# Layer 1's attention: the shared rotary key reaches the other key tiles by SBUF-to-SBUF transfers

## The chip, the cores and the metric

The kernel runs on one core of a Trainium2 chip. The metric is the device time of one execution in microseconds (us), the median of repeated runs. Engines are named as in the profile: PE is TensorE (matmuls and transposes), DVE is VectorE, ACT is ScalarE, POOL is GpSimd, and SP is SyncE, which only issues DMAs in this kernel.

## The reference

The model is a trunk of two layers over one sequence of 1024 tokens with 1024 features, all in float32. Layer 0 is a differential attention, layer 1 a multi-head latent attention (MLA); a gated MLP with a causal convolution follows each. The change touches layer 1's attention:

```python
proj = h @ w_in
c_q = rms_norm(proj[..., :MLA_Q_RANK], q_norm_g)
c_kv = rms_norm(proj[..., MLA_Q_RANK:MLA_Q_RANK + MLA_KV_RANK], kv_norm_g)
k_pe = apply_rope(proj[..., MLA_Q_RANK + MLA_KV_RANK:], cos, sin)
q = (c_q @ w_uq).reshape(b, s, MLA_HEADS, MLA_NOPE + MLA_ROPE)
q_pe = apply_rope(q[..., MLA_NOPE:], cos, sin)
kv = (c_kv @ w_ukv).reshape(b, s, MLA_HEADS, MLA_NOPE + MLA_V)
...
sc = (jnp.einsum('bqhd,bkhd->bhqk', qn, k_nope)
      + jnp.einsum('bqhr,bkr->bhqk', qp, k_pe)).astype(jnp.float32) * scale
```

There are 16 heads. Each has 64 key features of its own (`k_nope`), but the 32 rotary key features (`k_pe`) have no head index: all heads use the same ones. A chunk mask (chunks of 64 tokens) and a softmax follow, then the product with the values.

## The kernel before

**Parts of a number.** A float32 matmul operand is held as a high part (`hi`, L123 to L127: a cast to F32R, on ACT unless DVE is asked for) and a low part (`lo`, L130: the difference, on DVE unless POOL is asked for). `mm3` (L119 to L121) makes a product of three matmuls. Tiles live in named places of SBUF: `s0` to `s13` (8 KB in each partition), `u0` to `u15` (4 KB) and `h0` to `h13` (2 KB). A new tile in a place waits until the last user of the old one is done.

**The key tiles.** A key tile `kT[j]` has 128 partitions, and in each the high and the low part for 1024 tokens. Partitions 0 to 63 hold the head's own key features. Partitions 64 to 127 hold the rotary key, twice (64 to 95 and 96 to 127), which answers to the two rotated forms of the query in `q`. There are four tiles, in `s0`, `s11`, `s12` and `s8`; head n uses tile n mod 4. The own features are written anew for each pair of heads (`k_unit`), but the rotary half of a tile is written once and stays for all heads. `rotary` writes it into `kT[0]` from the rotated key, for one half of the tokens (512) at a time; `share(j, half)` then copies partitions 64 to 127 of such a half from `kT[0]` to `kT[j]`.

**Order of the stage.** `mla_input` runs over the eight token tiles of 128, and two rounds more: `latents(i)` makes the projections and norms of tile i (squares at L157, the root on POOL at L163, the norm at L1293), `turn` transposes them, `values` makes the values and writes them to DRAM (`v_d`). After round 5 `rotary(0)` turns the first half of the key, in round 8 `rotary(1)` turns the second. `heads.first` starts three products of the first pair of heads ahead of the last tile.

Then `steps` runs 64 attention steps, four for each head. A step t has two query blocks of 128; in most heads the four steps take the blocks in the order `p` = 1, 0, 3, 2, so that the first two need keys of the first half alone. Each step computes scores (into the two PSUM tiles `S`), their row maximum (L1625, DVE) and exponential (L1626, ACT), scales the probabilities (`weigh`, L1632 on DVE and L149 on POOL), transposes them (L248, PE) with a split into parts (L127 on ACT, L130 on DVE), and multiplies by the values (L1646 and L1647, PE) into the single PSUM bank `u`, which L1649 (ACT) and L1650 (DVE) empty into SBUF. The work of three steps overlaps. `prepare(t)` puts the fetches and splits of later heads' weights and values among the steps, and there the copies for tiles 2 and 3.

**What sets the order on the engines.** Outside regions that are scheduled by hand (`manual_schedule`, not used in this stage), a planner orders the instructions at build time: the kernel is built with `tile.TileContext(nc, schedule_with_timeline_sim=True)`. It follows a simulated timeline, in which an instruction that is ready earlier can go ahead of others written before it. So the written order is not the order in the queues: two of the copies that `prepare` writes at steps 3 and 5 run at 1326 and 1328 us, before the first exponential of step 0 at 1331.9 us. On the chip each engine works off its queue in the order fixed at build time, and an instruction whose inputs aren't ready holds up what is behind it.

Of the kernel before, what the change touches and what calls it, by code (L numbers as in the profile page):

```python
# [56 lines left out]
class Trunk:  # L57
# [1196 lines left out]
    def mla_input(self, W, hts, turns, v_d, heads_of):  # L1254


        nc, a = self.nc, self.a
# [11 lines left out]
        def latent_tiles(half):  # L1269
            for x, place in zip((cq, ckv), (("s2", "s3"), ("s6", "s7"))[half]):  # L1270
                pieces = self.at(place, [P, 4, 512], F32R)
                for part in range(2):
                    x[part].append(pieces[:, 2 * part : 2 * part + 2, :])
            for part in range(2):
                cq2[part].append(self.at(f"h{2 * half + part}", [P, 512], F32R))
# [7 lines left out]
        def latents(i):  # L1283
            acc = self.big()
            for k in range(KD):
                for b, m, kind in ((0, 384, "q"), (512, 288, "kv")):
                    wh, wl = where[kind, k]
                    self.mm3(acc[:, b : b + m], hts[i][:, 0, k, :], hts[i][:, 1, k, :], wh, wl, k == 0, k == KD - 1)
            nat = nats([P, 672])
            for b, m, off, gain in ((0, 384, 0, g[0]), (512, 256, 384, g[1])):  # L1290
                d = nat[:, off : off + m]
                r = self.rstd(acc[:, b : b + m], d, m)
                nc.vector.scalar_tensor_tensor(d, acc[:, b : b + m], r, gain, ALU.mult, ALU.mult)  # L1293
            nc.scalar.copy(nat[:, 640:672], acc[:, 768:800])
            return nat

        def turn(i, nat):
            half = i // 4
            s = slice((i % 4) * P, (i % 4 + 1) * P)
            ps = self.bank()  # L1300
            for j in range(3):
                nc.tensor.transpose(ps[:, j * P : (j + 1) * P], nat[:, j * P : (j + 1) * P], self.ident)
            v = ps.rearrange("p (k s) -> p k s", s=P)
            for dst, src in ((cq, v[:, 0:2]), (cq2, v[:, 2])):
                h, l = (x[half][:, s] if dst is cq2 else x[half][:, :, s] for x in dst)
                self.hi(h, src)
                self.lo(l, src, h)
            ps = self.bank()
            for j in range(2):
                nc.tensor.transpose(ps[:, j * P : (j + 1) * P], nat[:, (3 + j) * P : (4 + j) * P], self.ident)  # L1310
            nc.tensor.transpose(ps[:MLA_ROPE, 256:384], nat[:, 640:672], self.ident)
            v = ps[:, :256].rearrange("p (k s) -> p k s", s=P)
            self.hi(ckv[0][half][:, :, s], v)
            self.lo(ckv[1][half][:, :, s], v, ckv[0][half][:, :, s])
            nc.scalar.copy(kp[half][:, s], ps[:MLA_ROPE, 256:384])

        def values(i):
            half = i // 4
            s = slice((i % 4) * P, (i % 4 + 1) * P)
            vs = self.raw([P, D])  # L1320
            for b, y in ((0, self.bank("u")), (512, self.bank())):
                for k in range(2):
                    ch, cl = (cT.kv(part, half, k)[:, s] for part in range(2))
                    self.mm3(y, ch, cl, late.wv[k][0][:, b : b + 512], late.wv[k][1][:, b : b + 512], k == 0, k == 1)
                if b == 0:
                    heads.own(i, y[:, :P])
                nc.scalar.copy(vs[:, b : b + 512], y)
            nc.sync.dma_start(v_d[:, :, i].rearrange("h p e -> p h e"), vs.rearrange("p (h e) -> p h e", e=P))

        def fetch_tab(half):  # L1330
            late.tab = [self.at(place, [MLA_ROPE, 512]) for place in ("h12", "h13")]
            for x in range(2):
                nc.sync.dma_start(late.tab[x], a["rope_k"][:, x, half * 512 : (half + 1) * 512])

        def rotary(half):
            r = self.rope(rope, kp[half], *late.tab, MLA_ROPE // 2, MLA_ROPE)
            t = nats([MLA_ROPE, 2, 512], F32R)
            self.hi(t[:, 0, :], r[:MLA_ROPE])
            self.lo(t[:, 1, :], r[:MLA_ROPE], t[:, 0, :], nc.gpsimd)
            heads.rotary(half, t)  # L1340
# [3 lines left out]
        for i in range(NT + 2):  # L1344
            if readies:
                readies.pop(0)()
            if i == NT - 1:
                heads.share(1, 0)
                heads.first()
            if i < NT:  # L1350
                nat[i] = latents(i)
                if turns:
                    turns.pop(0)()
            if i in (1, 5):
                latent_tiles(i // 4)
            if i == 1:

                late.wv = [self.split(f"s{4 + k}", self.fetch(a["mla_wuv"][k * P : (k + 1) * P, :], D)) for k in range(2)]
                heads = heads_of(cT)
            if i == 4:  # L1360
                fetch_tab(0)
            if 0 <= i - 1 < NT:
                turn(i - 1, nat.pop(i - 1))
            if i >= 2:
                values(i - 2)
            if i == 5:
                rotary(0)
                fetch_tab(1)
            if i == NT:
                rotary(1)  # L1370
                heads.share(1, 1)
        return heads

    def mla_heads(self, cT, v_d, o_d):
        nc, a = self.nc, self.a
        pairs = MLA_HEADS // 2
        heads = [dict() for _ in range(MLA_HEADS)]
# [3 lines left out]
        k_places, kT = ["s0", "s11", "s12", "s8"], []  # L1381
# [6 lines left out]
        def fetch_w(p):  # L1388
            raws["w"] = self.fetch(a["mla_w"][p], D)
# [16 lines left out]
        def q_unit(h, half):  # L1406
            if half == 0:
                heads[h]["q"] = q_ring([P, 2, S], F32R)
            q = heads[h]["q"]
            acc = self.bank()  # L1410
            off = (h % 2) * 384
            for k in range(3):
                wh, wl = (w[:, off + k * P : off + (k + 1) * P] for w in W[h // 2])
                self.mm3(acc, wh, wl, cT.q(0, half, k), cT.q(1, half, k), k == 0, k == 2)
            yield
            s = slice(half * 512, (half + 1) * 512)
            t = t_ring([P, 512])
            nc.vector.tensor_mul(t, acc, cs[:, s])
            self.hi(q[:, 0, s], t)
            self.lo(q[:, 1, s], t, q[:, 0, s], nc.gpsimd if h > 1 else None)  # L1420

        def k_unit(p, half):
            acc = self.bank()
            for k in range(2):
                wh, wl = (w[:, 768 + k * P : 768 + (k + 1) * P] for w in W[p])
                self.mm3(acc, wh, wl, cT.kv(0, half, k), cT.kv(1, half, k), k == 0, k == 1)
            yield
            s = slice(half * 512, (half + 1) * 512)
            for j in range(2):
                k = heads[2 * p + j]["k"] = kT[(2 * p + j) % 4]  # L1430
                src = acc[j * 64 : j * 64 + 64]
                self.hi(k[0:64, 0, s], src)
                self.lo(k[0:64, 1, s], src, k[0:64, 0, s])

        def pair_units(p):
            return [
                lambda: k_unit(p, 0), lambda: k_unit(p, 1),
                lambda: q_unit(2 * p, 0), lambda: q_unit(2 * p, 1),
                lambda: q_unit(2 * p + 1, 0), lambda: q_unit(2 * p + 1, 1),
            ]  # L1440
# [3 lines left out]

        def first():

            self.run([u() for u in pair_units(0)[::2]])

        def own(i, y):
# [8 lines left out]
        def k_tiles(n):  # L1458
            kT.extend(self.at(place, [P, 2, S], F32R) for place in k_places[len(kT) : n])
# [5 lines left out]
            for x, r0 in enumerate((64, 96)):  # L1465
                self.hi(kT[0][r0 : r0 + 32, :, s], t, nc.vector if x else None)

        def share(j, half):
            k_tiles(j + 1)
            s = slice(half * 512, (half + 1) * 512)  # L1470
            self.hi(kT[j][64:128, :, s], kT[0][64:128, :, s])

        def prepare(t):
            p, u = divmod(t, 8)
            if t == 0:
                fetch_w(1)
            if t == 1:
                split_w(1)
                k_tiles(4)
            if 3 <= t < 7:  # L1480
                share(2 + (t - 3) // 2, (t - 3) % 2)
            for at, ahead, f in ((2, 1, fetch_v), (4, 1, split_v), (5, 2, fetch_w), (7, 2, split_w)):
                if u == at and p + ahead < pairs:
                    f(p + ahead)
            if t >= 4 * MLA_HEADS - 10:
                prefetch[0]()
# [439 lines left out]
```

## Time and profile before

| | |
|---|---|
| time, median of 3 runs | 2433.61 us (2432.45 to 2436.21) |
| the profiled execution's own time | 2437.63 us |
| its span in the profile | 2435.8 us |
| instructions | 32815 |
| DMA, mean over the span | 88 GB/s |
| HBM read, written | 159.37 MB, 52.43 MB |

The profile shows one execution. Its span runs from the first to the last instruction; its own time is 1.8 us longer. A timeline gives the start of an instruction from the start of the span, its length, its engine and line, the tile it writes and those it reads, and in brackets how long its engine stood idle before it and what ended that. Tiles `S`, `b` and `u` written by PE are PSUM tiles; the names `s`, `u` and `h` written by other engines are the places in SBUF, without their numbers.

### The profile page before, as it was taken

The numbers are of one execution on the slowest core, as the hardware profiler recorded it, in microseconds if no ns is written. First come the engines' busy times: TensorE is split into PE (matmuls) and PEld (weight loads), VectorE is DVE, ScalarE is ACT, GpSimd is POOL, SyncE is SP. The second block draws the span as 40 slices with busy tenths as digits, with TensorE's granted clock in tenths as the row PEclk, the third lists the DMA queues.
The fourth block names the chain that finished last, engine by engine and source line by source line (L and its number), as shares of the span: only waits on it lengthen the run. The fifth ranks groups of instructions, "written<-read, shape, count | busy, mean of one in ns | idle before, by whom it ended". The sixth has DMA issues, their size and how long they took to land. (4 is left out here: it accounts for less than half of the span.)

```text
span 2435.8 us, 32815 instructions
## 1 busy us (share of the span) xinstructions
PE 2366.7 (97%) x12032; PEld 2011.8 (83%) x12032; DVE 1901.7 (78%) x3091; ACT 1304.2 (54%) x2432; POOL 626.4 (26%) x500
## 2 busy tenths in 40 slices
PE   7999999999999999999999999999999999999998
PEld 6888787888888888878898789988888888887886
DVE  6667776856888888899964788886478888888997
ACT  5677777844444444444445777775344444444443
POOL 4545454425000000000042666664330000000001
PEclk9999999999999999999999999999999999999999
DMA  4101111233222222543221211123322222227502
GB/s 161 42 34 44 35 36 44 100 100 120 74 80 78 87 78 93 193 173 122 84 89 54 68 40 40 40 80 116 106 69 87 78 88 86 78 87 276 173 1 78
DMA packets 95505, 213.93 MB, mean 88 GB/s; under 512 B 8688, under 2 KB 33904, under 8 KB 95344
## 3 DMA queue, kind: packets, MB, share of 16 engines
q1 hardware_dynamic: 86448, 184.56, 22.6%
q10 hardware_dynamic: 8896, 27.27, 3.0%
q8 instruction: 95, 1.56, 0.3%
q14 instruction: 66, 0.54, 0.1%
HBM read 159.37 MB, written 52.43 MB: 87 GB/s over the span
## 5 line engine op out<-in xcount | busy, mean ns | idle before, releaser
L163 POOL TENSOR_TENSOR st<-st,mhalf 128x1 f32<-128x1 f32 x56 | 34.3, 614 | 1310.7 <-DVE st L162 1306.8
L127 ACT CAST u<-h 128x512 fp32r<-128x512 f32 (+2 forms) x242 | 146.1, 619 | 279.8 <-DVE h L771 259.9
L119 PE MATMUL S<-s,u 128*128 128x512 f32 (+1 forms) x752 | 286.6, 381 | 0.6 <-DVE s L130 0.5
L121 PE MATMUL S<-s,u 128*128 128x512 f32 (+1 forms) x752 | 285.1, 379 | 0.0
L120 PE MATMUL S<-s,u 128*128 128x512 f32 (+1 forms) x752 | 285.1, 379 | 0.0
L119 PE MATMUL b<-s,u 128*128 128x512 f32 x588 | 230.6, 392 | 2.1 <-DVE S L1624 1.0
L120 PE MATMUL b<-s,u 128*128 128x512 f32 x588 | 229.0, 389 | 0.0
L121 PE MATMUL b<-s,u 128*128 128x512 f32 x588 | 229.0, 389 | 0.0
L828 DVE SCALAR_TENSOR_TENSOR u<-u,conv,u 128x1023 f32<-128x1023 f32 (+1 forms) x176 | 225.0, 1278 | 1.9 <-ACT u L824 1.9
L149 POOL TENSOR_TENSOR u<-u,st 128x384 f32<-128x384 f32 (+7 forms) x160 | 169.7, 1070 | 149.1 <-DVE st L1632 107.2
L119 PE MATMUL u<-s,s 128*128 128x512 f32 (+1 forms) x440 | 177.8, 404 | 13.4 <-ACT h L552 7.1
L127 ACT CAST s<-u 128x512 fp32r<-128x512 f32 (+2 forms) x202 | 128.9, 673 | 101.8 <-PE u L121 36.0
L130 DVE TENSOR_TENSOR u<-b,u 128x512 fp32r<-128x512 f32 (+1 forms) x256 | 158.1, 630 | 29.7 <-ACT u L127 27.9
L121 PE MATMUL u<-s,s 128*128 128x512 f32 (+1 forms) x440 | 172.8, 393 | 0.0
L120 PE MATMUL u<-s,s 128*128 128x512 f32 (+1 forms) x440 | 172.2, 391 | 0.0
L119 PEld LDWEIGHTS S<-s,u 128*128 128x128 f32 x752 | 142.6, 190 | 27.6 <-DVE s L130 0.9
L120 PEld LDWEIGHTS S<-s,u 128*128 128x128 f32 x752 | 142.6, 190 | 26.3
L121 PEld LDWEIGHTS S<-s,u 128*128 128x128 f32 x752 | 142.5, 190 | 26.1
L127 ACT CAST u<-b 128x512 fp32r<-128x512 f32 (+1 forms) x256 | 133.6, 551 | 36.9 <-PE b L248 27.3
L831 ACT ACTIVATE u<-u 128x1024 f32<-128x1024 f32 x44 | 46.7, 1062 | 187.5 <-DVE u L828 187.5
L130 DVE TENSOR_TENSOR u<-h,u 128x512 fp32r<-128x512 f32 x166 | 114.1, 688 | 32.4 <-ACT u L127 31.5
L130 DVE TENSOR_TENSOR s<-u,s 128x512 fp32r<-128x512 f32 (+2 forms) x187 | 127.7, 717 | 11.7 <-ACT s L127 11.5
(260 smaller groups left out, 6641.7 us busy)
## 6 DMA issues: line engine op xcount, KB each, us to landing
u<-in_ffn_up SPq DMA_DIRECT2D x88, 512.0 KB, 3.9
g_d<-u ACTq DMA_DIRECT2D x44, 512.0 KB, 2.6
u<-in_ffn_down SPq DMA_DIRECT2D x66, 256.0 KB, 5.1
u<-g_d SPq DMA_DIRECT2D x62, 256.0 KB, 4.2
s<-in_da_wqkv SPq DMA_DIRECT2D x23, 512.0 KB, 3.2
x_d<-u SPq DMA_DIRECT2D x16, 512.0 KB, 2.9
s<-x_d SPq DMA_DIRECT2D x8, 1024.0 KB, 10.8
u<-o_d SPq DMA_DIRECT2D x24, 256.0 KB, 2.8
```

The source lines that it names most:

```text
L119: mm(out, lh, rl, start=first, stop=False, skip_group_check=onto)
L120: mm(out, lh, rh, start=False, stop=False, skip_group_check=onto)
L121: mm(out, ll, rh, start=False, stop=last, skip_group_check=onto)
L127: self.nc.scalar.copy(out, src)
L130: (eng or self.nc.vector).tensor_sub(out, src, hi.bitcast(F32))
L149: self.nc.gpsimd.tensor_mul(x, x, s.to_broadcast(list(x.shape)))
L163: nc.gpsimd.tensor_tensor(r, s, self.mhalf, ALU.pow)
L828: nc.vector.scalar_tensor_tensor(t[half][:, back:], u[half][:, : S - back], w, t[half][:, back:], ALU.mult, ALU.add)
L831: nc.scalar.activation(t[0], t[0], AF.Silu)
```

## The change

The six copies on ACT (three tiles, two halves of 512 tokens, 64 partitions by 2 x 512 elements each) are replaced by three transfers, one for each tile, of 64 partitions by 2 x 1024 elements, 512 KB each. They are issued by POOL (`nc.gpsimd.dma_start`). Since each covers all tokens, it comes after `rotary(1)`: that for tile 1 is written where the second half copy was, and those for tiles 2 and 3 at step 1, behind the split of the second pair's weights, instead of steps 3 to 6. The place of tile 1 is taken in `heads.first`, at the same point of the order as before; the places of tiles 2 and 3 are taken at step 1, as before.

```diff
@@ mla_input
             if i == NT - 1:
-                heads.share(1, 0)
                 heads.first()
...
             if i == NT:
                 rotary(1)
-                heads.share(1, 1)
+                heads.share(1)
@@ mla_heads
         def first():
 
+            k_tiles(2)
             self.run([u() for u in pair_units(0)[::2]])
...
-        def share(j, half):
+        def share(j):
             k_tiles(j + 1)
-            s = slice(half * 512, (half + 1) * 512)
-            self.hi(kT[j][64:128, :, s], kT[0][64:128, :, s])
+            nc.gpsimd.dma_start(kT[j][64:128], kT[0][64:128])
 
         def prepare(t):
...
             if t == 1:
                 split_w(1)
-                k_tiles(4)
-            if 3 <= t < 7:
-                share(2 + (t - 3) // 2, (t - 3) % 2)
+                share(2)
+                share(3)
```

## The prediction

> **What bounds the kernel now.** I read the page first, then the groups of instructions by form, then the stretch in which the changed lines run (by windows of 4 us, and as a timeline of each engine), then the DMA issues. Of the page:
>
> ```profile
> span 2435.8 us, 32815 instructions
> PE 2366.7 (97%) x12032; PEld 2011.8 (83%) x12032; DVE 1901.7 (78%) x3091; ACT 1304.2 (54%) x2432; POOL 626.4 (26%) x500
> s<-x_d SPq DMA_DIRECT2D x8, 1024.0 KB, 10.8
> ```
>
> PE is busy for 2366.7 of 2435.8 us. An edit that takes no work from PE can only win where PE stands idle or runs at a lower clock, 69 us in the whole span. The edit takes this group away from ACT, and nothing from PE:
>
> ```profile
> L127 ACT CAST s<-s 64x1024 fp32r<-64x1024 f32 x6 | 6.1, 1042 | 5.7 <-PE S L121 5.6
> ```
>
> That is 6.1 us on an engine with a share of 54%, so the share says "free". A share is an average, though, and the six copies all lie between 1310 and 1355 us. The windows of that stretch (columns: length, then busy us of PE, PEld, DVE, ACT and POOL with counts, then the granted PE clock, DMA share, GB/s) show a place where ACT is full and PE isn't:
>
> ```profile
> 1328.00:1332.00 4.00, 3.34 (x16) 2.42 (x16) 3.19 (x10) 3.94 (x13) 1.10 (x2) 1.00 0.00 0
> ...
> 1348.00:1352.00 4.00, 3.16 (x17) 2.29 (x15) 3.52 (x3) 3.95 (x6) 2.76 (x3) 1.00 0.27 108
> 1352.00:1356.00 4.00, 2.12 (x10) 1.51 (x10) 3.50 (x7) 3.91 (x6) 2.13 (x1) 1.00 0.59 184
> 1356.00:1360.00 4.00, 3.42 (x13) 2.83 (x14) 2.83 (x7) 3.92 (x8) 1.68 (x1) 0.68 0.20 80
> 1360.00:1364.00 4.00, 3.37 (x19) 2.53 (x17) 3.67 (x10) 2.37 (x5) 3.11 (x2) 0.89 0.14 33
> ```
>
> PE's idle time in these rows is 0.66 + 0.84 + 1.88 + 0.58 + 0.63 = 4.59 us, and the clock of 0.68 and of 0.89 in two of them costs at most 0.32 x 4 + 0.11 x 4 = 1.72 us more. So 6.3 us is about all that this edit can win here.
>
> **The copies that go.** The timeline of ACT (start, length, instruction, idle time before it and its releaser):
>
> ```profile
> 1310.41 1.04 ACT L127 CAST s<-s 64x1024 fp32r<-64x1024 f32 x1 [2.67 <-PE S L121]
> ...
> 1326.27 1.04 ACT L127 CAST s<-s 64x1024 fp32r<-64x1024 f32 x1 [2.96 <-PE S L121]
> 1327.34 0.49 ACT L157 ACTIVATE u<-S 128x384 f32<-128x384 f32 x1
> ...
> 1328.07 1.05 ACT L127 CAST s<-s 64x1024 fp32r<-64x1024 f32 x1
> ...
> 1349.16 1.04 ACT L127 CAST s<-u 32x1024 fp32r<-32x1024 f32 x1
> ...
> 1352.15 2.94 ACT L127 CAST s<-s 64x1024 fp32r<-64x1024 f32 x3
> 1355.11 0.48 ACT L127 CAST u<-b 128x384 fp32r<-128x384 f32 x1
> 1355.62 0.37 ACT L1649 COPY h<-u 64x256 f32<-64x256 f32 x1
> 1356.01 1.01 ACT L1626 ACTIVATE u<-S,st 128x896 f32<-128x896 f32 x1
> ```
>
> Only the first three copies (the first halves of the three key tiles) come early, each as soon as PE releases a slot. The three second halves follow the rotation of the second half (1349.16) and stand in a row of 2.94 us, ahead of three things that others wait for. PE and DVE at that place:
>
> ```profile
> 1350.26 0.44 PE L119 MATMUL S<-s,s 128*128 128x384 f32 x1 [0.59 <-ACT s L127]
> ...
> 1356.56 0.38 PE L1646 MATMUL u<-u,s 128*128 128x256 f32 x1 [2.29 <-DVE h L1650]
> ...
> 1361.27 0.44 PE L119 MATMUL S<-s,s 128*128 128x384 f32 x1
> ...
> 1361.90 1.55 PE L248 MATMUL b<-ident,u 128*128 128x128 f32 x10
> 1353.96 1.20 DVE L1625 TENSOR_REDUCE st<-S 128x1 f32<-128x1024 f32 x1
> 1355.62 0.56 DVE L130 TENSOR_TENSOR u<-b,u 128x384 fp32r<-128x384 f32 x1 [0.46 <-ACT u L127]
> 1356.10 0.40 DVE L1650 TENSOR_TENSOR h<-h,u 64x256 f32<-64x256 f32 x1
> ```
>
> The product at L1646 needs its one PSUM bank emptied, by L1649 on ACT and then L1650 on DVE. L1649 stands behind the three copies, so PE loses 2.29 us. Without them the cast of 1355.11 and L1649 could run 2.94 us earlier, L1649 at about 1352.7 to 1352.8. DVE then has to take L1650 before the reduce of 1353.96. That is likely, since L1650 belongs to an earlier step and was merely not ready; if DVE kept its order, L1650 would still follow the end of that reduce (1355.16) and the cast's partner at L130, and start at 1355.16 + 0.56 = 1355.7, a gain of 0.4 us. I take the 2.29 us.
>
> The two copies of 1326.27 and 1328.07 stand before and between the two squares (L157) of the last token tile. From those the path runs over the norm, the transposes and the rotation to the cast of 1349.16, on which PE waits 0.59 us at 1350.26. With 1.04 + 1.05 us taken out ahead of it I count these 0.59 us as gone, as the other queues on the way leave 2 us of room for it. The copy of 1310.41 delays squares too, but no PE idle time follows it: nothing.
>
> The lower clock stands in the two windows behind PE's emptiest one. If the idle time goes, I take half of the 1.72 us back, 0.86 us, because PE in those windows also waits for others and a faster PE would partly wait more.
>
> Sum of what goes: 2.29 + 0.59 + 0.86 = 3.74 us.
>
> **The transfers that come.** Three transfers of 64 partitions by 8 KB, 512 KB each, issued by POOL. The trace has neither a transfer from SBUF to SBUF nor one issued by POOL, so both the issue and the landing need bounds. POOL's timeline, an issue by SP, the group of issues of the same size in the stretch, and a DVE instruction beside POOL's:
>
> ```profile
> 1348.69 2.39 POOL L130 TENSOR_TENSOR s<-u,s 128x1024 fp32r<-128x1024 f32 x1 [0.59 <-ACT s L127]
> 1351.73 2.40 POOL L130 TENSOR_TENSOR u<-u,u 128x1024 fp32r<-128x1024 f32 x1 [0.65 <-ACT u L127]
> 1357.38 1.68 POOL L149 TENSOR_TENSOR u<-u,st 128x896 f32<-128x896 f32 x1 [3.25 <-DVE st L1632]
> 1360.30 3.11 POOL L149 TENSOR_TENSOR u<-u,st 128x1024 f32<-128x1024 f32 x2 [1.23 <-DVE st L1632]
> 1351.11 0.32 SPq L135 DMA_DIRECT2D u<-v_d  x1
> v_d<-u SPq DMA_DIRECT2D x5, 512.0 KB, 3.2
> 1349.17 2.46 DVE L130 TENSOR_TENSOR s<-h,s 128x512 fp32r<-128x512 f32 x1 [0.35 <-ACT s L127]
> ```
>
> Landing: between 3.2 us (512 KB to v_d) and 10.8 us (the slowest row, 1024 KB from x_d). I take 4 us, near the row of the same size. The first transfer can go only when both halves of the rotated key stand, at 1349.16 + 1.04 = 1350.20, and POOL is in an instruction until 1351.08. Today's half copy for head 1 was made at 1310; now all of head 1's scores wait for the transfer. These are the matmuls of 1361.27 (384 wide: head 1's first step), or about 1358 once the stall is gone. 1351.1 + 1 + 4 = 1356.1: hidden, with 2 us to spare. Heads 2 and 3 come four and eight steps later. Nothing.
>
> The Trainium skill (SBUF — State Buffer, "Door 1: The DMA port swizzle") says that partitions 64 to 127 reach only half of the DMA ports; with its 436 GB/s halved, 512 KB would take an estimated 2.4 us of moving, and with the 2 us of fixed cost that the skill (DMA: Bandwidth & Descriptors, "Anatomy of one DMA") names, 4.4 us. The sum would be the same by it; no row here shows a transfer within SBUF.
>
> Issue: between 0.32 us (one on SP) and 2.4 us (POOL's own large instruction). I take 1.0 us, nearer to the issue, because it computes nothing over the data. Queued behind these issues on POOL are the splits (L130, for weights needed later) and the scaling of the probabilities (L149), for which PE's transposes at 1361.90 wait: they begin 0.04 us after the first 1.56 us of the pair at 1360.30. POOL's room between 1351.08 and 1357.38, beside the one split, is 0.65 + 3.25 = 3.9 us today. With L149 ready 2.3 us earlier, 1.6 us of it is left; three issues take 3.0 us, so L149 is 1.4 us later than it could be, and PE with it. That is the price: 1.4 us. A gain on POOL is excluded, since nothing leaves its queue.
>
> Net: 3.74 - 1.4 = 2.3 us, in a profiled execution from a span of 2435.8 to 2433.5 us, and from 2437.6 to 2435.3 us with what lies around it. The profiled execution is 4.0 us above the median of the three timed runs, 2433.6; there I expect 2433.6 - 2.3 = **2431.3 us**, 0.1% faster. A measurement here tells about 0.2%, or 4.9 us, from no change, so this counts as no change.
>
> **The rivals.**
> - *All of it goes* (faster). The planner puts instructions in the order of a simulated timeline; with ACT free it may close the whole 4.59 us and the clock stays at 1.00. 2433.6 - 6.3 = 2427.3 us. For it: three engines wait on ACT in just these windows. Against it: DVE is at 3.5 of 4 us there as well and would be the next to be late. Chance 0.24.
> - *No gain.* DVE keeps the order of today (0.4 us instead of 2.29), or the transfer lands 10.8 us after 1351.1, at 1361.9, so that head 1's scores begin 0.6 us later than today. Either way about 2434 us. Chance 0.12.
> - *POOL becomes the late engine* (slower). Place: the three issues, ahead of L149 of the third step. At 2.4 us each they take 7.2 us, 3.3 us more than the room of today; PE's transposes of 1361.90 move by that, the gain is lost, and a longer stall lengthens the low clock by up to 1.7 us: +5.0 us, 2438.6. The gain is gone at (3.74 + 1.6) / 3 = 1.8 us for an issue; from 2.4 us it is slower by over 0.2%. For it: POOL's instructions do get long beside DVE's. The DVE subtraction of 1349.17 with two SBUF operands took 2.46 us while POOL's of 1348.69 ran, longer than the reduce of 1353.96 with its 1024 elements (1.20 us) though it has 512. Against it: the DVE instructions shown from 1353.96 on read an operand from PSUM (S, b, and the bank u), not two from SBUF. Chance 0.28.
>
> A rule of the Trainium skill speaks for this last case: its page SBUF — State Buffer ("The 'DVE blocks DMA' trap") says that POOL builds the descriptors of its transfers in software and can be locked out of a port that it shares with DVE while DVE runs a two-port form, so that the transfer stands still; it advises SP or ACT as issuers. The row of 1349.17 agrees that the two engines hold each other up.
>
> **How the numbers follow.** Forecast 0.36, all of it 0.24, no gain 0.12, POOL late 0.28. Faster by over 0.2%: 0.24. Within: 0.36 + 0.12 = 0.48. Slower: 0.28. The likeliest case's own range, from the issue at 1.8 us (no gain, 2433.6) to the issue at 0.5 us (all under the room, 2429.9), is 2429.9 to 2433.6. The range for eight in ten takes in the gain of 6.3 us and the loss of 5.0 us: 2426.5 to 2439.0.
>
> **What would show it.** Right: no CAST of 64x1024 on ACT (2432 - 6 instructions and 6 us less busy time); three issues on POOL's queue after the rotation, about 1 us each; the idle time of about 2.3 us before L1646 gone; the granted clock around 1356 to 1364 nearer to 1.00; no PE wait for a transfer at head 1's first scores. Wrong: issues of 2 us or more with L149 waiting behind them; PE idle with a DMA as releaser; or a change in PE's idle time outside 1310 to 1370 us, which would mean that a new order of the whole attention, and not these copies, made the difference.

## The result: slower by 5 us, with the profile after

| | before | after |
|---|---|---|
| median of 9 runs, same chip | 2434.85 us (2432.17 to 2436.66) | 2440.22 us (2438.17 to 2442.80) |
| ratio, 95% interval | | 1.0021 [1.0013, 1.0029] |

The kernel became slower by 0.2%. The forecast of 2431.3 us and its range, which ended at 2439.0 us, both missed. The profiled execution of after took 2440.22 us, its span 2438.4 us. From the page of after:

```profile
span 2438.4 us, 32798 instructions
PE 2365.6 (97%) x12032; PEld 2007.8 (82%) x12032; DVE 1902.5 (78%) x3091; ACT 1298.3 (53%) x2426; POOL 629.3 (26%) x503
q0 software_dynamic: 240, 1.57, 0.3%
```

The edit did what it says: ACT has six instructions and 5.9 us less, POOL three instructions more, and queue 0 moved 1.57 MB, the three transfers of 512 KB. At the place where the prediction looked, the change even does well. Windows of after, at the same times and with the columns of the prediction's (the stage starts 3.2 us earlier in this execution, so the work in them is a little further on):

```profile
1328.00:1332.00 4.00, 4.00 (x22) 3.25 (x21) 1.72 (x7) 2.74 (x8) 0.83 (x1) 1.00 0.44 131
...
1348.00:1352.00 4.00, 3.50 (x17) 2.62 (x18) 3.94 (x8) 3.63 (x8) 3.08 (x4) 1.00 1.10 262
1352.00:1356.00 4.00, 2.71 (x16) 2.21 (x16) 3.88 (x9) 2.49 (x6) 3.42 (x2) 1.00 1.13 203
1356.00:1360.00 4.00, 3.25 (x24) 2.70 (x23) 2.89 (x11) 3.19 (x8) 3.47 (x3) 1.00 0.85 217
1360.00:1364.00 4.00, 4.00 (x28) 3.62 (x27) 2.67 (x7) 2.03 (x6) 1.40 (x2) 1.00 0.00 0
```

PE's idle time in these five windows is 0 + 0.50 + 1.29 + 0.75 + 0 = 2.54 us where it was 4.59, the clock stays at 1.00 where it fell to 0.68, and ACT is no longer full. The timelines of POOL and PE there, and the view of the issuing line (durations in ns):

```profile
1346.81 1.75 POOL L1470 DMA_DIRECT2D s<-s  x3
1348.56 2.41 POOL L130 TENSOR_TENSOR u<-u,u 128x1024 fp32r<-128x1024 f32 x1
1351.89 3.53 POOL L149 TENSOR_TENSOR u<-u,st 128x896 f32<-128x896 f32 x2 [0.91 <-DVE st L1630]
```

```profile
1345.89 0.45 PE L119 MATMUL S<-s,s 128*128 128x384 f32 x1 [0.22 <-ACT s L127]
...
1351.79 0.39 PE L1644 MATMUL u<-u,s 128*128 128x256 f32 x1 [0.24 <-DVE h L1648]
...
1355.31 0.30 PE L248 MATMUL b<-ident,u 128*128 128x128 f32 x1 [1.05 <-DVE S L1622]
1355.43 0.41 PE L119 MATMUL S<-s,s 128*128 128x384 f32 x1
```

```profile
L1470 POOL DMA_DIRECT2D s<-s x3: 517/519/726, 1346.8 to 1348.0; - x3
...
DMA to landing us min/median/max: 7.0/8.8/10.6
```

(L1644, L1648, L1630 and L1624 of after are L1646, L1650, L1632 and L1626 of before: two lines fewer stand above them.) The stall of 2.29 us at the product with the values (L1646 of before), behind the three copies, is 0.24 us. The wait of 0.59 us for the cast of the rotated key is 0.22 us. The three issues take 1.75 us together, and L149 behind them waits for DVE, not for POOL. Head 1's first scores start at 1355.43, with no idle time of PE directly before them; by the landing of 7.0 us the first transfer stands at 1353.8. The idle time of 1.05 us that stands ahead, before the transposes of 1355.31, ended with DVE's work, not with a transfer: DVE is now the engine that is late here, busy for 3.94 and 3.88 of 4 us.

So the loss lies elsewhere. I cut the attention stage at instructions that both kernels have: its first copy of L1294, and the first exponentials of heads 1, 4 and 14, up to the last exponential. In us:

| | to head 1 | heads 1 to 3 | heads 4 to 13 | heads 14, 15 | sum | rest, to the end |
|---|---|---|---|---|---|---|
| before | 113.8 | 68.0 | 207.4 | 36.6 | 425.9 | 758.6 |
| after | 109.2 | 68.3 | 219.8 | 34.5 | 431.7 | 758.6 |
| PE idle, before | 5.13 | 2.02 | 1.23 | 1.46 | | |
| PE idle, after | 2.75 | 1.12 | 7.84 | 1.40 | | |

The head of the stage wins 4.6 us, and heads 4 to 13, in which neither kernel makes a copy or a transfer of the rotary key, lose 12.4 us. The sum, +5.8 us, is near the difference of the medians (+5.4). These are single executions, but the stretch of heads 4 to 13 hardly scatters: the five kernels below and above that have before's order there take 207.4 to 207.5 us. The window of that stretch, first before, then after:

```profile
1430.00:1640.00 210.00, 208.77 (x1366) 188.28 (x1365) 174.92 (x426) 163.02 (x355) 140.58 (x112) 1.00 0.16 47
```

```profile
1430.00:1640.00 210.00, 202.16 (x1286) 179.91 (x1285) 165.51 (x398) 151.78 (x331) 129.49 (x104) 0.99 0.15 44
```

Every engine does less in the same time, so no engine became the bound: they wait for each other. All of PE's waits from 1440 to 1640 us (us in total, times, longest), before and after:

```profile
PE b L119 <- DVE u L130: 0.4, 1, 0.4
PE b L119 <- DVE S L1624: 0.4, 1, 0.4
```

```profile
PE b L248 <- DVE u L130: 5.2, 9, 1.2
PE S L119 <- ACT u L1624: 1.8, 1, 1.8
```

Nine times in 200 us the transposes of the probabilities (L248) wait for DVE's subtraction L130, some 22 us apart, which is once for each head. One of them, with ACT and DVE beside it, in after's timelines:

```profile
1530.84 1.25 PE L248 MATMUL b<-ident,u 128*128 128x128 f32 x10
1531.85 0.36 PE L1644 MATMUL u<-u,s 128*128 128x256 f32 x1
...
1533.71 0.55 PE L248 MATMUL b<-ident,u 128*128 128x128 f32 x3 [1.21 <-DVE u L130]
```

```profile
1531.53 1.07 ACT L127 CAST u<-b 128x512 fp32r<-128x512 f32 x2 [1.23 <-PE b L248]
```

```profile
1531.33 0.96 DVE L1623 TENSOR_REDUCE st<-S 128x1 f32<-128x768 f32 x1 [0.46 <-DVE S L1622]
...
1532.50 0.56 DVE L1623 TENSOR_REDUCE st<-S 128x1 f32<-128x384 f32 x1
1532.98 1.28 DVE L130 TENSOR_TENSOR u<-b,u 128x512 fp32r<-128x512 f32 x2
```

And PE at the like place before:

```profile
1533.84 0.62 PE L248 MATMUL b<-ident,u 128*128 128x128 f32 x4
1534.22 0.42 PE L119 MATMUL S<-s,s 128*128 128x384 f32 x1
...
1534.83 0.60 PE L248 MATMUL b<-ident,u 128*128 128x128 f32 x4
1535.18 0.47 PE L119 MATMUL S<-s,s 128*128 128x512 f32 x1
...
1535.96 0.60 PE L248 MATMUL b<-ident,u 128*128 128x128 f32 x4
```

Up to four transposes fill one PSUM tile `b`, and there are three such tiles. Each is emptied by a cast on ACT and a subtraction on DVE. Before, PE fills one tile, makes scores while ACT and DVE empty it, and fills the next. After, PE makes the first transposes of two tiles ahead, one by one among scores, and then a row of ten, which completes these two and fills the third. The casts start at 1531.53, and DVE has two row maxima (L1623) ahead of its subtractions: those run from 1532.98 to 1532.98 + 1.28 = 1534.26. Behind four products PE's next instructions are transposes for a fourth tile; they start at 1533.71, when the first of the two subtractions is about done.

The order of the built queues shows how general this is. Before and after differ only in layer 1's attention, but there some 1690 instructions of PE, 553 of DVE, 352 of ACT and 88 of POOL stand in another place. Heads 4 to 13 have 360 instructions of L248. Before makes them in 76 runs of three or four, twelve of six to eight and none longer; after has 51 of three or four, 24 single ones, five of two, nine of six to eight and ten of nine to eleven, and each of these ten completes three tiles. Ten long runs in ten heads go with nine waits in 200 us, a little more than nine heads. The planner laid out most of the attention anew, up to head 13.

PE's idle time explains 7.84 - 1.23 = 6.6 of the 12.4 us. The other 5.8 us are in PE's busy time, in the groups that belong to the same steps. Heads 4 to 13, first before, then after:

```profile
L248 PE MATMUL b<-ident,u 128*128 128x128 f32 x352 | 53.5, 275 | 0.4 <-DVE S L1624 0.3
L1646 PE MATMUL u<-u,s 128*128 128x256 f32 x159 | 41.8, 292 | 0.0
```

```profile
L248 PE MATMUL b<-ident,u 128*128 128x128 f32 x357 | 56.9, 278 | 5.2 <-DVE u L130 5.2
L1644 PE MATMUL u<-u,s 128*128 128x256 f32 x160 | 44.7, 306 | 0.0
```

The transposes take 3.4 us more, the products of L1646 and L1647 together 4.1 us, and no other group changes by over 0.7 us (a few records are missing from each trace, more of them before). The granted clock of 0.99 in this stretch is worth an estimated 2 us of the 5.8. Why the rest comes with the new order stays open.

### The profile page after: what moved, and what is told of

Its sections match the earlier page's. It is cut to its first block, busy times and chain, and to the rows that moved or that the text cites. A ratio compares the mean times of both kernels' runs of the same rounds, so it can differ in the third digit from the quotient of the medians.

```text
span 2438.4 us, 32798 instructions
## 1 busy us (share of the span) xinstructions
PE 2365.6 (97%) x12032; PEld 2007.8 (82%) x12032; DVE 1902.5 (78%) x3091; ACT 1298.3 (53%) x2426; POOL 629.3 (26%) x503
## 3 DMA queue, kind: packets, MB, share of 16 engines
q0 software_dynamic: 240, 1.57, 0.3%
## 4 chain that ended last, share of the span: by engine, by line
PE 79%; DVE 9%; ACT 5%; DMA 3%; issue 2%; POOL 2%; SPq 0%; ACTq 0%; POOLq 0%; DVEq 0%
PE S L119 13%; PE S L121 13%; PE S L120 13%; PE b L121 8%; PE b L119 8%; PE b L120 8%; PE u L119 4%; PE u L120 3%; PE u L121 3%; PE b L248 2%; DVE s L130 1%; PE u L1645 1%; PE u L1644 1%; DVE st L1623 1%; PE b L182 1%
## 5 line engine op out<-in xcount | busy, mean ns | idle before, releaser
L149 POOL TENSOR_TENSOR u<-u,st 128x384 f32<-128x384 f32 (+7 forms) x160 | 169.5, 1067 | 145.5 <-DVE st L1630 105.8
L130 DVE TENSOR_TENSOR u<-b,u 128x512 fp32r<-128x512 f32 (+1 forms) x256 | 158.2, 631 | 32.5 <-ACT u L127 30.5
L248 PE MATMUL b<-ident,u 128*128 128x128 f32 x864 | 137.0, 276 | 8.2 <-DVE u L130 5.9
L130 DVE TENSOR_TENSOR u<-h,u 128x512 fp32r<-128x512 f32 x166 | 114.1, 687 | 32.4 <-ACT u L127 31.5
```

What stands on the lines that cost most here:

```text
L130: (eng or self.nc.vector).tensor_sub(out, src, hi.bitcast(F32))
L149: self.nc.gpsimd.tensor_mul(x, x, s.to_broadcast(list(x.shape)))
L248: self.nc.tensor.transpose(ps[:, j * P : (j + 1) * P], probs[t][:, k : k + P], self.ident)
```

## The experiments

Two theories. **Order**: the loss comes from the planner's new order of the ten middle heads, and would come without any transfer; the transfers themselves win. **Transfers**: the three transfers cost the time, by POOL's issues, by their landing or by what they disturb. Single times of one kernel differ by up to 8 us between executions (a kernel below had 2432.0 to 2440.4 us), so I read medians with their intervals, and stages. The runs came in two sets, each with the kernel before beside it (2435.99 us in the first, 2436.33 in the second).

To hold an order, edges between neighbours of each queue are given to the planner; they order but do not wait:

```diff
     with tile.TileContext(nc, schedule_with_timeline_sim=True) as tc:
         kernel_body(tc, aps, out)
+        hold(tc)    # tc.add_manual_dep(next, previous, NoSync) along ORDER
```

**hold_old: after's transfers, in before's order** (PE, ACT, DVE and POOL, in layer 1's attention).

> The kernel after, with its three transfers, but the queues of PE, ACT, DVE and POOL in the attention held in the order of the kernel before (order edges between neighbours; nothing else changes). Theory ORDER (the loss is the new order of the attention steps that the planner made, the transfers themselves are a gain): the PE idle time of 1430 to 1640 us falls from 7.8 us to about 1 us, and the copies' stall is gone, so 2430 to 2433 us, faster than before. Rival TRANSFER (issue on POOL and landing of the transfers make the loss, whatever the order): 2438 to 2441 us, as the kernel after.

Measured: 2435.68 us, ratio 1.0002 [0.9993, 1.0011]. The stretch of heads 4 to 13 and PE's waits there:

```profile
1430.00:1640.00 210.00, 208.16 (x1361) 187.50 (x1360) 174.67 (x426) 162.98 (x355) 140.70 (x112) 1.00 0.18 55
```

```profile
PE b L248 <- DVE u L130: 0.6, 1, 0.6
```

The loss of after is gone with the same three transfers in place (207.5 us in heads 4 to 13). The gain that I expected is a miss. The stretch to head 1 takes 112.4 us, 1.4 less than before and the whole stage 2.1 less, and nothing of it shows in the median. Its timeline says why:

```profile
1352.85 0.39 PE L1646 MATMUL u<-u,s 128*128 128x256 f32 x1 [1.73 <-DVE h L1650]
```

With DVE in the order of before, this matmul waits for the same L1650, 1.73 us instead of 2.29.

**copies_new: before's copies, in after's order.** The kernel is before's, with the same `hold(tc)` and the order of after's four queues.

> The kernel before, with its six copies on ACT, but the same four queues held in the order of the kernel after. ORDER: the steps from 1430 us on have about 7 us of PE idle time as in the kernel after, and ACT is burdened with the copies on top: 2440 to 2446 us. TRANSFER: no transfer, no loss: 2433 to 2436 us.

Measured: 2446.24 us, ratio 1.0043 [1.0030, 1.0056], at the upper end of what ORDER expected.

```profile
1430.00:1640.00 210.00, 202.05 (x1298) 179.48 (x1297) 168.13 (x408) 153.47 (x338) 131.11 (x106) 1.00 0.15 44
```

```profile
PE b L248 <- DVE u L130: 5.2, 9, 1.2
```

A kernel without a single one of the transfers shows after's loss, in the same nine waits: heads 4 to 13 take 218.1 us, 10.7 more than before. The clock is 1.00 in this stretch, so the clock isn't its cause. To head 1 it takes 114.0 us at a granted clock of 0.97 (before 113.8 us at 0.99; late_copies below, in before's order, 115.0 us at 0.97): as long as the copies are on ACT, the new order wins there no more than the scatter. PE then waits at another instruction, for an exponential:

```profile
1357.56 0.80 PE L119 MATMUL S<-s,s 128*128 128x512 f32 x1 [2.81 <-ACT u L1626]
```

**sync_transfers: after, but SP issues the transfers.**

```diff
-            nc.gpsimd.dma_start(kT[j][64:128], kT[0][64:128])
+            nc.sync.dma_start(kT[j][64:128].bitcast(F32), kT[0][64:128].bitcast(F32))
```

> The kernel after with the three transfers issued by SP instead of POOL (as plain float32 bytes); the planner's order stays nearly that of the kernel after (10 of 12033 PE places differ). ORDER: 2439 to 2441 us, as after, though the transfers land sooner (3 to 5 us instead of 8.8 us). TRANSFER, if it is POOL's issue: about 2434 us or less.

Measured: 2441.91 us, ratio 1.0027 [1.0017, 1.0037]. The view of the issuing line:

```profile
L1471 SPq DMA_DIRECT2D s<-s x3: 524/588/2018, 1348.3 to 1349.5; - x3
...
DMA to landing us min/median/max: 4.4/7.2/9.0
```

POOL issues nothing here and the time is that of after (heads 4 to 13: 219.4 us). POOL's issues are not the cause. The time is 0.9 us above the range that I gave for ORDER, and only the first landing lies in the 3 to 5 us.

**late_copies: after, with copies on ACT where the transfers are written.**

```diff
-            nc.gpsimd.dma_start(kT[j][64:128], kT[0][64:128])
+            for s in (slice(0, 512), slice(512, 1024)):
+                self.hi(kT[j][64:128, :, s], kT[0][64:128, :, s])
```

> Copies on ACT as in the kernel before, but written at the places where the kernel after writes its transfers (both halves of tile 1 behind the second rotation, tiles 2 and 3 at step 1); the planner makes a third order. ORDER: the time goes with the order that comes out, so the PE idle time of 1430 to 1640 us differs from 1.2 us without any transfer; from the two orders seen, 2432 to 2442 us. TRANSFER: 2434 to 2436 us, since no transfer is there and ACT carries the same six copies.

Measured: 2436.86 us, ratio 1.0003 [0.9994, 1.0012]; to head 1 115.0 us, heads 4 to 13 207.4 us. The third order that I expected did not come: the built queues of PE, DVE, ACT and POOL are those of before, place for place, the six copies included. So the written place alone turns nothing over. The run tells nothing more between the two theories, but as a second execution of before's order it shows the scatter of the stages: 1.1 us in the stretch to head 1, under 0.1 us in heads 4 to 13.

**one_transfer and two_transfers: which transfer turns the order over?** The first moves tile 1 by a transfer and copies tiles 2 and 3; the second copies tile 1 and moves tiles 2 and 3 (diffs against before).

```diff
@@ one_transfer, round 8
-                heads.share(1, 1)
+                heads.move(1)    # nc.gpsimd.dma_start(kT[1][64:128], kT[0][64:128])
```

```diff
@@ two_transfers, prepare
-            if 3 <= t < 7:
-                share(2 + (t - 3) // 2, (t - 3) % 2)
+                for j in (2, 3):    # under t == 1
+                    nc.gpsimd.dma_start(kT[j][64:128], kT[0][64:128])
```

> Tile 1 alone by a transfer on POOL, tiles 2 and 3 by copies on ACT as in the kernel before; the planner is free. In its order for heads 4 to 13 the transposes of PE stand in runs of up to 11, as in the kernel after (seven runs of 9 or more; the kernel before has none). ORDER: about 7 us of PE idle time from 1430 to 1640 us, 2440 to 2444 us. TRANSFER: a third of the loss, 2436 to 2438 us.

> Tiles 2 and 3 by transfers on POOL, tile 1 by its two copies on ACT; the planner is free, and its order for heads 4 to 13 has the runs of transposes of the kernel before (none over 8). ORDER: PE idle from 1430 to 1640 us about 1 us, and some of the copies' stall gone: 2433 to 2436 us. TRANSFER: two thirds of the loss, 2438 to 2440 us.

Measured: 2443.27 us, 1.0034 [1.0021, 1.0046], and 2434.34 us, 0.9992 [0.9983, 1.0000]. The windows of the ten heads, in this order:

```profile
1430.00:1640.00 210.00, 202.47 (x1299) 180.14 (x1299) 167.84 (x407) 153.77 (x339) 130.55 (x106) 1.00 0.15 44
```

```profile
1430.00:1640.00 210.00, 206.52 (x1342) 184.94 (x1341) 172.23 (x419) 159.51 (x350) 138.20 (x110) 1.00 0.17 52
```

Tile 1's transfer alone brings the order with the long runs of transposes and its whole loss; the other two don't (heads 4 to 13: 217.9 and 209.4 us). On PE, one_transfer's built queue has after's order in heads 4 to 13, place for place, with ten runs of nine or more and not seven. two_transfers has one run of nine there and not none, and loses 2.0 us against before.

**mix and mix_sync: after's order until the start of head 2, before's from there on.** The second also issues from SP, as above. If the order is the cause, the gain at the head should stay and the loss go.

> The kernel after with its transfers; PE, ACT, DVE and POOL held in the order of the kernel after up to the beginning of head 2, and in the order of the kernel before from there. ORDER: the gain of 4.6 us that the kernel after has at head 1's first exponential stays to the end, and the steps from 1430 us on lose nothing: about 0.998 of the kernel before, 2430 to 2432 us, the fastest of all. TRANSFER: as the kernel after, 1.002.

> The same held order as mix, the three transfers issued by SP instead of POOL. If POOL's issue (1.75 us for three) or the late landing costs anything, this is 1 to 2 us faster than mix; if they are hidden, the same within 1 us.

Measured: 2433.96 us, 0.9992 [0.9983, 1.0001], and 2432.21 us, 0.9985 [0.9976, 0.9994].

| us | to head 1 | heads 1 to 3 | heads 4 to 13 | heads 14, 15 | sum |
|---|---|---|---|---|---|
| mix | 110.0 | 69.5 | 207.4 | 36.3 | 423.1 |
| mix_sync | 109.5 | 69.5 | 207.5 | 36.6 | 423.1 |

The head's gain stays (3.8 and 4.3 us) and the loss is gone. 1.5 us go where the two orders meet, in heads 1 to 3 (69.5 us against 68.0), so mix gives less than I expected of it. mix_sync is faster than both kernels, by 0.15% against before. The two differ by 0.5 us to head 1, but after and mix, which have one order up to there, differ by 0.8 us; their medians stand 1.75 us apart with intervals that overlap, so whether SP is the better issuer stays open.

## Why the prediction was wrong

By its own steps:

- **The copies that go: right in mechanism and about right in sum, not in each term.** Of the stall of 2.29 us, 2.05 went; of the 0.59 us, 0.37. The clock stays at 1.00 where half of the loss was counted as won. The prediction's own argument against a larger gain, that DVE would be the next to be late, came true: PE waits 1.05 us for it. The head of the stage won 4.6 us, between the net of 2.3 us and the cap of 6.3 us; two executions of one order differ by up to 1.1 us there.
- **The price of the issues: too high.** Three issues took 1.75 us and not 3 us, and the 1.4 us that was to be lost behind them did not appear: L149 waited 0.91 us for DVE's L1630. That PE's transposes waited for L149 was assumed: the row of 1361.90 shows no idle time. The range of 0.5 to 1.8 us for one issue held (0.52 to 0.73).
- **The landing: too low, without effect.** 7.0 us for the first and up to 10.6 us for the third, against 4 us taken and bounds of 3.2 to 10.8. It was hidden all the same, with 1.6 us to spare where 2 were expected. The Trainium skill (DMA: Bandwidth & Descriptors, "Anatomy of one DMA") led to an estimate of 4.4 us; that section is on transfers issued by POOL, and POOL's 7.0 us does not agree with it. SP's first transfer took 4.4 us.
- **"DVE keeps the order of today": a real mechanism, put in the wrong case.** It was counted under *no gain*, with 0.4 us. hold_old shows it: with the old order the wait at L1646 shrinks by 0.56 us (2.29 to 1.73), the stage by 2.1 us, and the median by nothing that it can tell. The gain to head 1 needs both, the free ACT and a new order around it: 112.4 us with transfers in the old order, 114.0 us with copies in the new one, 109.2 us with transfers in the new one.
- ***POOL becomes late*: right in sign, wrong in mechanism.** sync_transfers takes POOL's issues out and is as slow. The Trainium skill (SBUF — State Buffer, "The 'DVE blocks DMA' trap") was cited for this rival; no run here isolates it, and the row of 1349.17, given for it, shows a DVE instruction that is long beside POOL's and not POOL's beside DVE's. POOL's issues took 0.52 to 0.73 us in windows where DVE was busy for 3.8 to 3.94 of 4 us, so the issues were not held up; but a transfer that stands still would show in the landing, and why POOL's first landed 2.6 us later than SP's no run tells.
- **The step that failed is the net.** It took 3.74 - 1.4 us from the span and with that held the rest of the stage's 425.9 us as it was, though the prediction says itself, in *all of it goes*, that the planner places instructions by a simulated timeline. It used that only as a source of gain, near the copies. A new order of the whole attention stands among the signs of a wrong prediction, but it had no chance and no price of its own. It cost 12.4 us in heads 4 to 13, of which 2.1 us came back in the last two heads; copies_new, without any transfer, lost 10.7 us in the same ten heads.

The four kernels that cross the two causes, as ratios to the before that was measured beside each (the two held kernels in one set, after in the first measurement):

| | before's order | after's order |
|---|---|---|
| copies on ACT | 1 | 1.0043 [1.0030, 1.0056] |
| transfers from POOL | 1.0002 [0.9993, 1.0011] | 1.0021 [1.0013, 1.0029] |

The order costs 0.4% with copies and 0.2% with transfers; the transfers are worth about 0.2% in the new order and nothing that can be told in the old one. So it is shown that the new order makes the loss. Not settled: why the planner, given the transfer of tile 1, bunches the transposes until head 13. one_transfer shows that it does, not why. That the bunches, and nothing else in the new order, make the whole loss is argued from the waits and covers 6.6 of 12.4 us; an order with the bunches alone taken apart was not tried.

## What to carry to other kernels

Where a planner orders the queues, an edit need not stay local: moving one tile by a transfer turned most of the attention over here, while moving the issues to SP or the copies to another written place left nearly every instruction where it was. Compare the order of every queue before and after, and look for long runs of one producer (here transposes) against the few tiles that its consumers empty, before costing the instructions that changed. Price the repeated stretch first: a new order that costs 1.2 us a head over ten heads outweighed the 4.6 us that the stage's entry won. To test an edit by itself, hold the old order and add the edit, then hold the new order without it; an edit that opens room may still need a new order around its own place to use it.

## What the hardware showed that was not expected

A transfer of 512 KB from SBUF to SBUF (64 partitions) landed 7.0 us after its issue on POOL where it was alone (one_transfer), and three in a row after 7.0, 8.8 and 10.6 us, in this order. From SP the first of three landed after 4.4 us. The row of that size on which the prediction leaned, to v_d, had 3.2 us; another on before's page, from in_x, had 7.9 us. An issue took 0.52 to 0.73 us on POOL; SP's three took 0.52 to 2.02 us. And one build of this kernel scatters by up to 8.4 us between executions (2432.0 to 2440.4 us, hold_old), more than the change that was to be measured.
